# Attention scores of two heads: one product over 128 rows, or two of 64 rows side by side

## The chip, the cores and the metric

The kernel runs on one core of one Trainium2 chip, in one launch. The metric is the device time of an execution in microseconds (us). TensorE multiplies: it loads a tile of weights (stationary) and streams columns of the other operand past it, into PSUM banks of 2 KB per partition. VectorE, ScalarE and GpSimd work on the results; SyncE issues the DMAs. Each engine runs its own queue in order and waits on semaphores for the others.

## What is computed

The reference is a stack of two attention layers followed by two layers of a mixer and a feed-forward part, for one sequence of 256 tokens with 1024 channels. Only the attention layers matter here. Each has three kinds of attention with 64 channels a head: 4 heads that see a selection of keys (dsa), 6 heads with a decay by cumulated gates (fox), and 6 heads that are used three times, on compressed, selected and windowed keys (nsa; the compressed branch is computed elsewhere).

```
s = jnp.einsum("bthd,bshd->bhts", qb, k).astype(jnp.float32) * scale
s = s + cb[:, :, :, None] - cum[:, :, None, :]        # fox only
p = masked_softmax(s, causal)
return jnp.einsum("bhts,bshd->bthd", p.astype(v.dtype), v)
```

All attention is causal, so the first 128 queries see 128 keys and the second 128 see 256.

## The kernel before, in words

`attend` does one pair of heads: 2 calls for dsa, 3 for fox and 6 for nsa (two branches of three pairs) in each layer, 22 calls in all. The queries of both heads lie stacked on 128 partitions, 64 channels each. The keys `kp` are laid out as a block diagonal of `[128, 2, 256]`: head 0 has its keys on rows 0 to 63 of its half and zeros below, head 1 zeros above and its keys on rows 64 to 127. One product of 128 rows thus gives both heads' scores next to each other in one PSUM bank.

A call goes through two token blocks `tb`. For each: the score product (L813; 256 columns for block 0, 512 for block 1, float32, two records each in the trace since a float32 product is made in two passes); for fox the decay (L816, one product per head); the mask as a bfloat16 product with the identity (L818, or L821 for dsa with its own mask); the row maximum of both heads in one VectorE instruction (L823); an exponential with its row sum on ScalarE for each head (L826); the reciprocal and the scaling on VectorE (L827, L831); transposes of the probabilities on TensorE (L835) and their copy to SBUF (L836). After both blocks come the products with the values (L839, L841), two heads in the two column halves of the array. The scores use the PSUM tag `s`, which has two banks; block 0 takes one and block 1 the other, and `turn` (L803) and the norm (L586) use the same tag.

Around this stand the projections of the layer: 16 units of `w_in` (L457, L458, L462 and L493: each weight is split into a high and a low part by ScalarE, L436, and VectorE, L437, and multiplied in three products) and then `w_out` (L510). They do not depend on the attention, so a scheduler in the recording layer puts them between the steps of `attend`; it decides by priorities and its own costs in which order instructions stand in each engine's queue. On the chip the queues then run in that order whatever the times. `self.after` adds an order between two instructions without a wait.

Lines used below that are not about scores: L1586 is a product of 64 rows in the mixer's recurrence, L1123 one in the compression of keys, and L412 with `oht` a product of 64 rows in the expert stage; L1162, L919 and L657 are small products near the attention.

Of the kernel before, what the change touches and what calls it, by code (L numbers as in the profile page):

```python
# [15 lines left out]
AF = mybir.ActivationFunctionType  # L16
ALU = mybir.AluOpType
AX = mybir.AxisListType
# [264 lines left out]
class Net:  # L283
# [522 lines left out]
    def attend(self, o, q, kp, vs, bias=None, first=True, last=True, cum=None, gate=None):  # L806

        nc = self.nc
        pt = self.hw.tile([128, 2, 384], F32, name="pt", tag="pt")
        for tb in range(2):  # L810
            K = 128 * (tb + 1)
            s = self.psum("s")[:, :2 * K].rearrange("p (a k) -> p a k", a=2)
            nc.tensor.matmul(s, q[:, tb * 128:tb * 128 + 128], kp[:, :, :K], start=True, stop=False)  # L813
            if cum is not None:
                for a in range(2):
                    nc.tensor.matmul(s[:, a], self.onehot(cum + a), self.cumt[:, :K], start=False, stop=False)  # L816
            if bias is None:
                nc.tensor.matmul(s[:, :, K - 128:], self.identb, self.mask[:, None].to_broadcast([128, 2, 128]), start=False,  # L818
                                 stop=True)
            else:  # L820
                nc.tensor.matmul(s, self.identb, bias[tb], start=False, stop=True)  # L821
            st = self.sm.tile([128, 6], F32, name="st")
            nc.vector.tensor_reduce(st[:, 0:2], s, axis=AX.X, op=ALU.max, negate=True)  # L823
            p = self.hw.tile([128, 2, K], F32, name="p", tag=f"p{tb}", bufs=2)
            for a in range(2):
                nc.scalar.activation(p[:, a], s[:, a], AF.Exp, bias=st[:, a:a + 1], accum_out=st[:, 2 + a:3 + a])  # L826
            nc.vector.reciprocal(st[:, 4:6], st[:, 2:4])  # L827
            if gate is not None:
                nc.vector.tensor_tensor(st[:, 4:6], st[:, 4:6], gate[:, tb], op=ALU.mult)
            for a in range(2):  # L830
                nc.vector.tensor_scalar(p[:, a], p[:, a], st[:, 4 + a:5 + a], None, op0=ALU.mult)  # L831
            pp = self.psum("t")[:, :2 * K].rearrange("p (a k) -> p a k", a=2)
            for a in range(2):
                for kb in range(tb + 1):
                    nc.tensor.transpose(pp[:, a, kb * 128:kb * 128 + 128], p[:, a, kb * 128:kb * 128 + 128], self.ident)  # L835
            nc.scalar.copy(pt[:, :, tb * 128:tb * 128 + K], pp)  # L836
        for a in range(2):
            r = slice(64 * a, 64 * a + 64)
            nc.tensor.matmul(o[r, :], vs[a](0), pt[:, a, 0:256], start=first, stop=False, skip_group_check=True,  # L839
                             tile_position=(0, 64 * a))  # L840
            nc.tensor.matmul(o[r, 128:256], vs[a](1), pt[:, a, 256:384], start=False, stop=last,  # L841
                             skip_group_check=True, tile_position=(0, 64 * a))
# [1369 lines left out]
```

## Time and profile before

| | us |
|---|---|
| median of 3 runs (lowest to highest) | 1862.64 (1861.03 to 1862.64) |
| the profiled execution, its own time | 1859.58 |
| its span, first to last instruction | 1857.7 |
| TensorE matmul busy in the span | 1788.7 |
| VectorE busy | 1069.8 |
| ScalarE busy | 873.2 |

A matmul's duration in the trace runs from its start to the end of its way through the array, and the next one starts earlier; what a product costs in the queue is therefore read from one start to the next. Weight loads have rows of their own (PEld) and overlap products. The two attention layers lie at about 0 to 235 us and 240 to 425 us, the score products from 97 to 211 and from 265 to 396; the last 800 us are the expert stage, which streams its weights by DMA.

### The profile page before, as it was taken

The page shows a single profiled execution, that of the slowest core. Times are in us where ns is not written, and L with a number is a line of the kernel's source. Part 1 is how long each engine was busy: PE and PEld are TensorE (multiplying, and loading weights), DVE is VectorE, ACT ScalarE, POOL GpSimd, SP SyncE. Part 2 cuts the span into 40 slices and gives each one's busy share as a digit, 9 for nine tenths or more (in the row PEclk, how much of TensorE's full clock was granted, in tenths as well). Part 3 has the DMA queues.
Part 4 walks back from the last instruction along what each step waited for, and adds up shares of the span by engine and source line. Part 5 has one row for each costly group of instructions (what it writes and reads, how often), then busy time and mean ns, then how long its engine had stood idle before and what let it go on. Part 6 is the DMA issues. An engine that isn't in the chain of part 4 may idle for free. (4 is left out here: it accounts for less than half of the span.)

```text
span 1857.7 us, 27558 instructions
## 1 busy us (share of the span) xinstructions
PE 1788.7 (96%) x11038; PEld 1357.8 (73%) x11038; DVE 1069.8 (58%) x1570; ACT 873.2 (47%) x1295; POOL 33.1 (2%) x78
## 2 busy tenths in 40 slices
PE   7999999999999999999999999888999999999996
PEld 5777788778897999888977876665666565656552
DVE  3765688757644655466437855645556555646532
ACT  3455475545463444355446754444444444544421
POOL 1000010000000000000000000000000000000000
PEclk9999999999999999999998999989999999999998
DMA  9664443234211555543137989999999999999996
GB/s 387 252 227 162 180 160 125 69 115 171 92 68 58 193 182 182 182 149 114 46 114 291 343 343 420 421 420 421 421 419 415 420 421 420 416 421 421 410 386 263
DMA packets 71175, 497.71 MB, mean 268 GB/s; under 512 B 8226, under 2 KB 9538, under 8 KB 11264
## 3 DMA queue, kind: packets, MB, share of 16 engines
q1 hardware_dynamic: 70752, 495.39, 67.9%
q8 instruction: 89, 1.46, 0.3%
q0 software_dynamic: 288, 0.48, 0.1%
q14 instruction: 46, 0.38, 0.1%
HBM read 493.81 MB, written 1.05 MB: 266 GB/s over the span
## 5 line engine op out<-in xcount | busy, mean ns | idle before, releaser
L437 DVE TENSOR_TENSOR raw<-raw,whi 128x2048 fp32r<-128x2048 f32 (+1 forms) x161 | 288.7, 1812 | 183.0 <-ACT whi L436 182.1
L436 ACT CAST whi<-raw 128x2048 fp32r<-128x2048 f32 (+1 forms) x188 | 287.1, 1552 | 155.8 <-PE mm L458 48.6
L412 PE MATMUL mm<-room,fx 128*64 128x512 f32 (+1 forms) x560 | 177.8, 535 | 12.1 <-DMA room<-in_mup_dram 6.3
L457 PE MATMUL mm<-xhi,whi 128*128 128x256 f32 x720 | 182.1, 288 | 0.7 <-ACT whi L436 0.7
L412 PE MATMUL mm<-whi,gh 128*128 128x512 f32 x448 | 177.7, 397 | 3.6 <-DVE y L2004 2.0
L458 PE MATMUL mm<-xlo,whi 128*128 128x256 f32 x720 | 180.4, 286 | 0.0
L412 PE MATMUL mm<-raw,fx 128*64 128x512 f32 (+1 forms) x544 | 171.9, 531 | 7.2 <-DMA raw<-in_mup_dram 7.2
L412 PE MATMUL mm<-whi,gl 128*128 128x512 f32 x448 | 174.9, 390 | 0.0
L436 ACT CAST whi<-room 128x2048 fp32r<-128x2048 f32 (+1 forms) x84 | 148.9, 1788 | 34.5 <-PE s L412 10.4
L457 PEld LDWEIGHTS mm<-xhi,whi 128*128 128x128 f32 x720 | 137.8, 191 | 8.1 <-issue 5.6
L458 PEld LDWEIGHTS mm<-xlo,whi 128*128 128x128 f32 x720 | 137.8, 191 | 1.5 <-issue 1.4
L412 PE MATMUL s<-whi,mh 128*128 128x512 f32 x448 | 116.5, 402 | 0.0
L412 PEld LDWEIGHTS s<-whi,mh 128*128 128x128 f32 x448 | 82.3, 188 | 35.5 <-issue 17.5
L462 PE MATMUL mm<-xhi,raw 128*128 128x256 f32 x720 | 104.6, 285 | 0.0
L412 PEld LDWEIGHTS mm<-room,fx 128*64 128x64 f32 (+1 forms) x560 | 54.5, 131 | 67.8 <-issue 44.1
L412 PEld LDWEIGHTS mm<-whi,gh 128*128 128x128 f32 x448 | 84.2, 188 | 21.5 <-issue 4.6
L412 PEld LDWEIGHTS mm<-whi,gl 128*128 128x128 f32 x448 | 84.2, 188 | 16.8
L412 PEld LDWEIGHTS mm<-raw,fx 128*64 128x64 f32 (+1 forms) x544 | 52.0, 131 | 59.5 <-issue 42.7
L462 PEld LDWEIGHTS mm<-xhi,raw 128*128 128x128 f32 x720 | 93.7, 192 | 1.2 <-DVE cin L1218 0.9
L1933 ACT CAST mh<-t 128x512 fp32r<-128x512 f32 x28 | 16.4, 586 | 159.6 <-PE t L415 159.6
L437 DVE TENSOR_TENSOR room<-room,whi 128x2048 fp32r<-128x2048 f32 x32 | 73.3, 2290 | 29.2 <-ACT whi L436 28.0
L412 PE MATMUL o<-room,msg 128*64 128x512 f32 (+1 forms) x536 | 85.5, 508 | 1.0 <-DVE msg L1928 1.0
(585 smaller groups left out, 3323.0 us busy)
## 6 DMA issues: line engine op xcount, KB each, us to landing
room<-in_mdown_dram SPq DMA_DIRECT2D x79, 1024.0 KB, 16.6
room<-in_mup_dram SPq DMA_DIRECT2D x54, 1024.0 KB, 17.0
room<-in_mgate_dram SPq DMA_DIRECT2D x53, 1024.0 KB, 13.9
raw<-in_mgate_dram SPq DMA_DIRECT2D x44, 1024.0 KB, 16.2
raw<-in_mup_dram SPq DMA_DIRECT2D x41, 1024.0 KB, 15.5
raw<-in_win_dram SPq DMA_DIRECT2D x29, 1024.0 KB, 6.3
raw<-in_din_dram SPq DMA_DIRECT2D x24, 1024.0 KB, 4.9
raw<-in_ada_dram SPq DMA_DIRECT2D x22, 1024.0 KB, 10.9
```

The costliest lines, as they stand in the source:

```text
L412: return self.kept(self.nc.tensor.matmul(*a, **k))
L436: a = nc.scalar.copy(h[:, v], r[:, v])
L437: b = nc.vector.tensor_tensor(lo[:, v], r[:, v], h[:, v].bitcast(F32), op=ALU.subtract)
L457: nc.tensor.matmul(out, w, xh[:, k], start=start and i == 0, stop=False)
L458: nc.tensor.matmul(out, w, xl[:, k], start=False, stop=False)
L462: nc.tensor.matmul(out, lo[:, off + i * 128:off + i * 128 + 128], xh[:, k], start=False, stop=stop and i == n - 1)
L1933: i = nc.scalar.copy(hh, pt), nc.vector.tensor_tensor(hl, pt, hh.bitcast(F32), op=ALU.subtract)
```

## The change

Each head gets a product of its own with 64 rows: head 0 on rows 0 to 63 of the array, head 1 on rows 64 to 127, without the zeros of the block diagonal. Each head has a PSUM bank of its own, which holds block 0 in columns 0 to 127 and block 1 in columns 128 to 383, so both banks belong to one call from its first product to its last exponential. Masks become one product a head, maxima one instruction a head, and each exponential follows its head's maximum.

```
+        ss = [self.psum("s") for _ in range(2)]
+        opened = [None, None]
         for tb in range(2):
             K = 128 * (tb + 1)
-            s = self.psum("s")[:, :2 * K].rearrange("p (a k) -> p a k", a=2)
-            nc.tensor.matmul(s, q[:, tb * 128:tb * 128 + 128], kp[:, :, :K], start=True, stop=False)
-            if cum is not None:
-                for a in range(2):
-                    nc.tensor.matmul(s[:, a], self.onehot(cum + a), self.cumt[:, :K], start=False, stop=False)
-            if bias is None:
-                nc.tensor.matmul(s[:, :, K - 128:], self.identb, self.mask[:, None].to_broadcast([128, 2, 128]), start=False,
-                                 stop=True)
-            else:
-                nc.tensor.matmul(s, self.identb, bias[tb], start=False, stop=True)
+            s = [t[:, 128 * tb:128 * tb + K] for t in ss]
+            for a in range(2):
+                r = slice(64 * a, 64 * a + 64)
+                m = nc.tensor.matmul(s[a], q[r, tb * 128:tb * 128 + 128], kp[r, a, :K], start=tb == 0, stop=False,
+                                     tile_position=(64 * a, 0), skip_group_check=True)
+
+                self.after(m, opened[a])
+                opened[a] = m
+            for a in range(2):
+                if cum is not None:
+                    nc.tensor.matmul(s[a], self.onehot(cum + a), self.cumt[:, :K], start=False, stop=False,
+                                     skip_group_check=True)
+                if bias is None:
+                    nc.tensor.matmul(s[a][:, K - 128:], self.identb, self.mask, start=False, stop=True, skip_group_check=True)
+                else:
+                    nc.tensor.matmul(s[a], self.identb, bias[tb][:, a], start=False, stop=True, skip_group_check=True)
             st = self.sm.tile([128, 6], F32, name="st")
-            nc.vector.tensor_reduce(st[:, 0:2], s, axis=AX.X, op=ALU.max, negate=True)
             p = self.hw.tile([128, 2, K], F32, name="p", tag=f"p{tb}", bufs=2)
             for a in range(2):
-                nc.scalar.activation(p[:, a], s[:, a], AF.Exp, bias=st[:, a:a + 1], accum_out=st[:, 2 + a:3 + a])
+                nc.vector.tensor_reduce(st[:, a:a + 1], s[a], axis=AX.X, op=ALU.max, negate=True)
+                nc.scalar.activation(p[:, a], s[a], AF.Exp, bias=st[:, a:a + 1], accum_out=st[:, 2 + a:3 + a])
```

The new lines shift those below by nine (L835 becomes L844). In the changed kernel the score product is L818, the decay L825, the masks L828 and L830, the maximum L834, the exponential L835, the transposes L844.

The first place is TensorE's queue at the first dsa call of layer 0. Before, both blocks' products and masks stand together:

```order
L493 MATMUL mm<-whi,xlo 128x256 x5
L813 MATMUL s<-kp_dk,q_dq_695 128x256
L821 LDWEIGHTS identb
L821 MATMUL s<-dsab_677,identb 128x256
L813 MATMUL s<-kp_dk,q_dq_695 128x512
L821 LDWEIGHTS identb
L821 MATMUL s<-dsab_680,identb 128x512
L493 MATMUL mm<-whi,xlo 128x256 x3
```

The same place of the changed kernel on TensorE:

```order
L493 MATMUL mm<-whi,xlo 128x256 x5
L818 MATMUL s<-kp_dk,q_dq_695 128x128 x2
L830 LDWEIGHTS identb
L830 MATMUL s<-dsab_677,identb 128x128
L830 LDWEIGHTS identb
L830 MATMUL s<-dsab_677,identb 128x128
L493 MATMUL mm<-whi,xlo 128x256 x3
L493 MATMUL mm<-raw_1140,xhi 128x256 x5
L818 MATMUL s<-kp_dk,q_dq_695 128x256 x2
L844 MATMUL t<-lead,p 128x128 x2
L830 LDWEIGHTS identb
L830 MATMUL s<-dsab_680,identb 128x256
```

Both heads' products are next to each other (x2); block 1 has moved behind eight projection products, and block 0's transposes stand between its products and its masks.

The second place is TensorE's queue at block 1 of the windowed branch of the first nsa pair. Before:

```order
L835 MATMUL t<-lead,p 128x128 x2
L458 MATMUL mm<-xlo,whi 128x256
L813 MATMUL s<-keys,q_rq_1217 128x512
L818 LDWEIGHTS identb
L818 MATMUL s<-mask,identb 128x2x128
```

The same call and block in the changed kernel:

```order
L462 MATMUL mm<-xhi,raw_1667 128x256 x6
L818 MATMUL s<-keys,q_rq_1223 128x256
L844 MATMUL t<-lead,p 128x128 x4
L818 MATMUL s<-keys,q_rq_1223 128x256
L828 LDWEIGHTS identb
L828 MATMUL s<-mask,identb 128x128
L828 LDWEIGHTS identb
L828 MATMUL s<-mask,identb 128x128
L462 MATMUL mm<-xhi,raw_1667 128x256 x2
```

Here the two heads' products are apart, with four transposes of full size between them.

## Rows read from the trace of the kernel before

**Rows 1.** The windows: length, then busy time (instructions) by engine, clock, DMA share, GB/s.

```profile
core 0: us, PE busy (x) PEld busy (x) DVE busy (x) ACT busy (x) POOL busy (x), PEclk, DMA share, GB/s
95.00:220.00 125.00, 123.63 (x953) 97.67 (x953) 78.16 (x159) 65.62 (x161) 0.00 (x0) 1.00 0.51 192
260.00:425.00 165.00, 163.03 (x1138) 134.72 (x1136) 119.92 (x284) 92.02 (x212) 1.70 (x3) 1.00 0.33 112
425.00:1060.00 635.00, 624.33 (x4137) 549.21 (x4135) 366.05 (x607) 312.08 (x524) 15.19 (x19) 0.98 0.43 154
1060.00:1857.00 797.00, 759.69 (x3878) 477.97 (x3876) 423.29 (x316) 343.26 (x290) 2.56 (x3) 0.98 0.97 402
```

**Rows 2.** The waits of TensorE in 95:425: total us, times, longest; first and last.

```profile
PE s L813 <- ACT q_fq L1029: 0.9, 2, 0.7
...
PE o L839 <- ACT pt L836: 0.2, 1, 0.2
```

**Rows 3.** The timeline of TensorE at the first call: start, length, instruction.

```profile
97.15 0.67 PE L813 MATMUL s<-kp_dk,q_dq 128*128 128x256 f32 x2
97.66 0.27 PE L821 MATMUL s<-dsab,identb 128*128 128x256 bf16 x1
97.77 1.02 PE L813 MATMUL s<-kp_dk,q_dq 128*128 128x512 f32 x2
98.63 0.38 PE L821 MATMUL s<-dsab,identb 128*128 128x512 bf16 x1
```

**Rows 4.** The timeline of one block 0 from mask to exponential, in 207.3:209.2.

```profile
207.10 0.39 PE L816 MATMUL s<-cumt,lead 128*128 128x128 f32 x2
...
207.32 0.27 PE L818 MATMUL s<-mask,identb 128*128 128x256 bf16 x1
...
207.63 0.42 DVE L823 TENSOR_REDUCE st<-s 128x2 f32<-128x256 f32 x1 [0.50 <-PE s L818]
...
208.09 0.37 ACT L826 ACTIVATE p<-s,st 128x128 f32<-128x128 f32 x1 [0.37 <-DVE st L823]
...
208.45 0.36 ACT L826 ACTIVATE p<-s,st 128x128 f32<-128x128 f32 x1
```

**Rows 5.** The timeline of TensorE in the expert stage, around 1493.5.

```profile
1493.53 1.20 PE L412 MATMUL mm<-my,oht 64*128 64x512 f32 x8
```

**Rows 6.** The timeline of TensorE around a product of 64 rows, 561.24:562.9.

```profile
561.24 0.39 PE L510 MATMUL mm<-whi,xhi 128*128 128x512 f32 x1
561.47 0.40 PE L510 MATMUL mm<-raw,xhi 128*128 128x512 f32 x1
561.79 0.48 PE L1586 MATMUL s<-vn,kbd 64*128 64x128 f32 x2
562.21 0.73 PE L510 MATMUL mm<-whi,xlo 128*128 128x512 f32 x2
562.78 0.40 PE L510 MATMUL mm<-whi,xhi 128*128 128x512 f32 x1
```

**Rows 7.** The timeline of TensorE around another, 86.8:88.1.

```profile
86.54 0.52 PE L493 MATMUL mm<-raw,xhi 128*128 128x256 f32 x3
86.90 0.28 PE L493 MATMUL mm<-whi,xhi 128*128 128x256 f32 x1
87.11 0.40 PE L1123 MATMUL t<-ch,cw 64*128 64x30 f32 x2
87.44 0.85 PE L493 MATMUL mm<-whi,xhi 128*128 128x256 f32 x5
```

**Rows 8.** Groups of weight loads in 95:425: busy us, mean ns, idle before.

```profile
L457 PEld LDWEIGHTS mm<-xhi,whi 128*128 128x128 f32 x224 | 42.7, 191 | 2.9 <-issue 1.9
...
L835 PEld LDWEIGHTS t<-lead,p 128*128 128x128 f32 x132 | 14.8, 140 | 9.8 <-issue 5.0 <-ACT pt L836 3.1 <-PE s L818 0.8
```

**Rows 9.** Line L818 by itself, the mask's weight load: ns min/median/max.

```profile
L818 PEld LDWEIGHTS <-identb x36: 97/98/181, 127.9 to 393.6; 128*128 128x128 bf16 x36
```

**Rows 10.** Line L823 by itself, the maxima: ns min/median/max.

```profile
L823 DVE TENSOR_REDUCE st<-s x44: 415/546/693, 98.0 to 394.2; 128x2 f32<-128x256 f32 x22, 128x2 f32<-128x512 f32 x22
```

**Rows 11.** VectorE's costliest group in 95:425, the weight split.

```profile
L437 DVE TENSOR_TENSOR raw<-raw,whi 128x2048 fp32r<-128x2048 f32 x35 | 80.1, 2289 | 42.5 <-ACT whi L436 42.5
```

## Prediction

> **What bounds the kernel now.** I read the windows first, since the change touches only the two attention layers. In the two stretches that hold their score products TensorE is busy 123.63 of 125.00 us and 163.03 of 165.00 us at a granted clock of 1.00, while VectorE is busy 78.16 and 119.92 and DMA moves at 0.51 and 0.33 of its share [rows 1]. So TensorE bounds these stretches and the other engines stand beside it. The table of waits says the same from the other side: in 95:425 TensorE's named waits are eight lines, from 0.9 us down to 0.2 us, 4.7 us in all [rows 2]. TensorE runs in order and has hardly a hole there, so a nanosecond added to its queue is a nanosecond added to the kernel. Behind these layers lie a stretch where TensorE is busy 624.33 of 635.00 us, and the expert stage, where DMA has 0.97 of its share [rows 1]. That stage cannot take back a late start: its loads go into buffers that earlier work frees, and moved by a later start they end as much later. I count TensorE's change in full.
>
> **What goes.** One attend has a score product for token block 0 (256 columns) and one for block 1 (512 columns). From the start of each to the start of the mask behind it: 97.15 to 97.66, 0.51 us, and 97.77 to 98.63, 0.86 us [rows 3]. 22 attends: 22 x 1.37 = 30.1 us go.
>
> **What comes: the products themselves.** A 64-row product of one head has half the columns. Two passes over 128 columns take 0.22 us (207.10 to 207.32 [rows 4]), two over 256 take 0.43 us (half of 0.86 [rows 3]). If the two heads stand next to each other in TensorE's queue they can run at once: in the expert stage eight records of 64 rows and 512 columns, on two row halves, take 1.20 us [rows 5], where 0.23 us apart, as full products start (561.24, 561.47 [rows 6]), they would need 1.8 us. I take the second head at 0.01 us for its start. Bounds: 0 and its full length.
> But the heads are next to each other in only half of the places. Counting score products in the changed queue: of the 44 pairs of heads 8 of block 0 and 13 of block 1 stand side by side; the other 23 are split by a mask, by transposes or by projection products (the second place shown under the change has four transposes in between). That leaves 36 uses of 0.22 us (8 pairs, 28 singles) and 31 of 0.43 us (13 pairs, 18 singles): 7.9 + 13.3 + 0.2 = 21.4 us.
>
> **What comes: switching the array.** Every one of these 67 groups is an island of 64-row work in a queue of 128-row work, and the trace shows the price. L1586 is a float32 product of 64 rows and 128 columns alone between full products. From 561.47 to 562.78 [rows 6] lie three full products (0.23 us each, as from 561.24 to 561.47) and L1586's own two passes (0.22 us): 0.91 us of work in 1.31 us. The island costs 0.40 us over its work: 0.09 before it, 0.20 from its start to the next full product, 0.11 on that product, whose weight load nothing hides. A second island is near it: from 86.90 to 87.44 [rows 7] lie one product of 0.12 us (86.54 to 86.90 holds three) and two passes of 30 columns, 0.05 us by L1586's width: 0.37 us over the work, and then the late load.
> What follows an island here is mostly the mask, whose bfloat16 weight load is short: 98 ns [rows 9] against 191 for a float32 one [rows 8]; these 36 cost 0.40 - 0.09 = 0.31 us. 16 are followed by a transpose (load of 140 ns [rows 8]: 0.35 us), the other 15 by float32 loads (0.40 us): mean 0.34 us. An island with its mask behind is not in the trace; its bounds are 0.1 (the entry wait alone) and 0.5 (the second island's price, rounded up). Islands of other shapes (values, gates, compressed keys) were there before: counting every change of tile size from shortly before the first score product to past the last one gives 94 before and 221 now. So 127 changes are new, 63.5 islands: 63.5 x 0.34 = 21.6 us.
> The Trainium skill, "TensorEngine Tiling (Array Packing)", Key Properties, says that changing the tiling mode drains TensorE, which is the rule that speaks against this change; it gives no price, and rows 6 do. The same page, Theoretical Speedup, gives up to 2x for a contraction of 64 rows or fewer; that alone would bring half of the 30.1 us, 15 us, and has its place among the rivals.
>
> **What comes: masks.** Two mask products of 128 columns replace one of 256: 0.11 us in either form (97.66 to 97.77 [rows 3]). But a half mask of 0.055 us covers only half of the 0.11 us that the next float32 weight load takes; where such a load follows (some 53 times) 0.055 us shows: 2.9 us. Bounds 0 and 5.
>
> **What comes: waits.** Block 1 now writes into the banks that block 0's exponentials read, so a bank is one round of mask, maximum, exponential. From rows 4: mask at 207.32, maximum at 207.63, which at half the width takes 0.29 us in place of 0.42 (an estimate from 0.42 and 0.69 for the two widths [rows 10]), exponential 0.37, so 1.0 us for the first head and, 0.36 later, 1.4 for the second; with 256 columns 1.25 and 1.75. What stands between on TensorE is mostly 8 projection products (0.96 us), transposes or value products. Laid end to end with the row times, four places come up short, 0.7 us in all. A weight split of 2.29 us on VectorE [rows 11] in front of a maximum can lengthen it; the projection products queued behind the waiting score product on TensorE, and ScalarE's and VectorE's later work on them, then wait as well. I take 2 us, bounds 0 and 12 (0.27 us a round).
> **Beside other work.** 44 more maxima on VectorE: 22 x (0.42 + 0.69) = 24 us become 44 x (0.29 + 0.42) = 31 us. VectorE is busy 0.63 to 0.73 of these stretches [rows 1], so TensorE hides the 7 us; without that cover they would be the price. The exponentials are the same in number and size. DMA issues, GpSimd and all stages after attention keep their order.
>
> **Sum.** -30.1 + 21.4 + 21.6 + 2.9 + 2 = +17.8 us. The profiled execution took 1859.58 us (span 1857.7), so 1877.4 by its own clock; the median of the runs is 3.1 us above it, and 1862.6 + 17.8 gives **1880 us**. The island decides the size: each 0.1 us of its price is 6.4 us.
>
> **Rivals.** (A) Switching to row halves waits for nothing: islands cost no more than their work. Then the sum is -30.1 + 21.4 + 2.9 + 2 = -4 us: 1859, a little faster; it turns slower once an island costs over 0.06 us. This is the skill page's speedup as far as the queue allows it (15 us only if all 44 pairs stood side by side). For it: rows 5, where halves overlap well. Against it: rows 6 and 7, the same shape of island in this same program.
> (B) The halves don't overlap in float32, whose products have two passes each with its own weight load: 8 x 0.22 + 13 x 0.43 = +7 us more, 1888. For it: rows 6 show one half at a time only, and rows 5 are one-pass products. Against it: rows 5 interleave several loads on both halves.
> (C) The bank round becomes the bound: in each attend block 1 waits out most of block 0's 1.4 us because weight splits stand in front: 22 x 1.2 = 26 us in place of 2, 1904. For it: maxima and splits share VectorE's queue, and a split takes 2.29 us [rows 11]. Against it: rows 2, where the waits that the queue had planned for came to 0.9 us at most.
> (D) The expert stage takes the delay back: it lives on DMA (0.97 [rows 1]), and if its loads start by themselves, TensorE's late arrival costs nothing: 1863. For it: DMA has only 0.43 of its share in the stretch before, room to run ahead. Against it: the loads need buffers that TensorE empties, and TensorE is busy 759.69 of 797.00 us in that stage too, so it has little to catch up with.
>
> **Chances.** Forecast 0.75 (own range 1872 to 1888), B 0.08, C 0.07, A 0.05, D 0.05. The range 1868 to 1891 takes in B and most of the bounds on the island (0.2 to 0.5 us) and leaves out A, C and D. A measurement of this kernel tells 0.2%, 3.7 us, from no change: faster 0.03 and same 0.07 (A on both sides of that line, and D), slower 0.90.
>
> **What would show it.** In the changed profile a lone score product of 128 columns should stand some 0.5 us from what precedes it to what follows beyond its neighbours' usual spacing, and two heads in a row should start within 0.02 us of each other. The attention stretches should be longer by 7 to 11 us each with TensorE as busy as before, the stages behind unchanged in length. VectorE's maxima rise to 88 without TensorE waiting for them. I am wrong if an island costs under 0.2 us, if TensorE's named waits before score products grow to over 5 us, or if the stages behind absorb the delay.

## The result, and the profile after

The changed kernel took 1876.93 us (median of four runs, 1872.33 to 1881.01) where the kernel before took 1861.84 beside it (1860.90 to 1862.64). The ratio is 1.0082 [1.0065, 1.0099]: 15.1 us slower. Forecast were +17.8 us and slower, with 1868 to 1891 as the range.

The profiled execution of the changed kernel is the longest of its four runs (1881.01 us, span 1879.2). The windows of both kernels, cut at the same places of the program (the transposes of the norm behind the first attention layer, the mixers' first product behind the second, the start of the expert stage), say where the time went. Columns: stretch, length, TensorE busy (instructions), granted clock, DMA share, GB/s. The kernel before:

```profile
core 0: us, PE busy (x), PEclk, DMA share, GB/s
95.00:230.51 135.51, 133.69 (x996) 1.00 0.52 194
230.51:429.53 199.02, 195.06 (x1373) 1.00 0.36 123
429.53:1070.17 640.64, 630.70 (x4167) 0.98 0.44 155
1070.17:1857.70 787.53, 749.52 (x3823) 0.98 0.98 404
```

The changed kernel:

```profile
core 0: us, PE busy (x), PEclk, DMA share, GB/s
95.00:238.11 143.11, 142.29 (x1060) 1.00 0.50 183
238.11:444.93 206.82, 203.00 (x1439) 1.00 0.34 118
444.93:1087.07 642.14, 632.21 (x4168) 0.97 0.44 155
1087.07:1879.20 792.13, 752.42 (x3823) 0.97 0.97 401
```

The first attention layer is 7.6 us longer and the second 7.8, 15.4 us together, at a clock of 1.00 (2.4 GHz) in both kernels. The stages behind do the same work (4167 and 3823 instructions, one record more or less); their 1.5 and 4.6 us came at a granted clock of 0.97 for 0.98. The other three runs of this kernel were 2 to 9 us shorter, and its median is 15.1 us behind, so I take these 6 us for what single executions differ by. The nine profiled executions bear that out: from the mixers' first product to the end they take 1427.8 to 1434.3 us, 1428.0 in the kernel that comes latest to it (heads apart, below) and 1432.9 in one whose TensorE work is that of before (maxima a head). The length of TensorE's stretch less its busy time, summed over both layers, was 1.82 + 3.96 = 5.8 us and is 0.82 + 3.82 = 4.6.

The waits of TensorE in 95:440 (total us, times, longest), which answer to [rows 2]; all six lines together make 3.8 us, and none names a score product:

```profile
PE s L586 <- DVE n L583: 1.1, 2, 0.6
PE o L493 <- ACT whi L436: 0.7, 1, 0.7
...
PE s L803 <- DVE rot L793: 0.3, 1, 0.3
```

Two heads side by side, in the timeline of TensorE around 130 us, answer to [rows 3]; the second fence is one of the places where they don't run at once, with the exponential that frees the bank (the last two rows are from narrow windows, where only the passes in the window are counted). PEld is TensorE's weight loader, and ACTIVATION_READ_ACCUMULATOR is the reading of the exponential's row sum.

```profile
129.44 0.39 PE L657 MATMUL mm<-raw,crep 128*32 128x256 f32 x3
129.76 0.49 PE L818 MATMUL s<-keys,q_rq 64*128 64x128 f32 x4
130.18 0.23 PE L828 MATMUL s<-mask,identb 128*128 128x128 bf16 x1
```

```profile
113.21 0.28 PE L458 MATMUL mm<-xlo,whi 128*128 128x256 f32 x1
113.33 0.37 ACT L835 ACTIVATE p<-s,st 128x128 f32<-128x128 f32 x1 [0.41 <-DVE st L834]
113.42 1.12 PE L818 MATMUL s<-kp_dk,q_dq 64*128 64x256 f32 x4
113.60 0.19 ACT L835 ACTIVATION_READ_ACCUMULATOR p<-s,st 128x1 f32 x1
...
114.47 0.10 PEld L830 LDWEIGHTS <-identb 128*128 128x128 bf16 x1 [0.33 <-issue]
...
113.42 0.70 PE L818 MATMUL s<-kp_dk,q_dq 64*128 64x256 f32 x2
113.84 0.70 PE L818 MATMUL s<-kp_dk,q_dq 64*128 64x256 f32 x2
```

At 129.76 all four passes of both heads are over in 0.42 us (to the mask at 130.18); the two heads' first passes start 6 ns apart. At 113.42 head 0 makes both of its passes alone and head 1 starts at 113.84. That is 0.05 us after the end, at 113.79, of block 0's exponential, which began at 113.33 and reads the bank that head 1 is to write. The pair takes 1.05 us to the mask instead of 0.63 for a pair of this width that runs at once. Of the 21 pairs that stand side by side in the queue, 14 start within 0.03 us of each other and 7 lie 0.2 to 0.42 us apart.

The score product's line by itself, loads and products, and what ended the idle time of the weight loader before it (us, times; two of the lines):

```profile
L818 PEld LDWEIGHTS s<-keys,q_rq x96: 182/184/187, 129.8 to 371.6; 64*128 64x128 f32 x96
L818 PE MATMUL s<-keys,q_rq x96: 272/375/480, 129.8 to 371.9; 64*128 64x128 f32 x48, 64*128 64x256 f32 x48
...
  issue: 4.8, 22
  ACT p L835: 1.7, 7
```

The maxima, by width (busy us, mean ns, idle before), answer to [rows 10]:

```profile
L834 DVE TENSOR_REDUCE st<-s 128x1 f32<-128x256 f32 x44 | 17.3, 419 | 14.3 <-PE s L828 12.7 <-PE s L830 1.3
L834 DVE TENSOR_REDUCE st<-s 128x1 f32<-128x128 f32 x44 | 12.1, 287 | 21.0 <-PE s L828 16.6 <-PE s L830 4.2
```

### The profile page after: what moved, and what is told of

The parts are those of the page before. It is cut to its first block, busy times and chain, and to the rows that moved or that the text cites. A ratio compares the mean times of both kernels' runs of the same rounds, so it can differ in the third digit from the quotient of the medians.

```text
span 1879.2 us, 27855 instructions
## 1 busy us (share of the span) xinstructions
PE 1809.6 (96%) x11170; PEld 1367.3 (73%) x11170; DVE 1074.9 (57%) x1614; ACT 875.5 (47%) x1295; POOL 33.1 (2%) x78
## 3 DMA queue, kind: packets, MB, share of 16 engines
HBM read 493.81 MB, written 1.05 MB: 263 GB/s over the span
```

## Experiments

The theory was the prediction's sum: a piece of 64-row work between 128-row work (an island) costs some 0.34 us beyond its work, and the overlap of the heads brings back less. The rivals were that the two heads don't overlap, that the time lies in the other parts of the edit (more instructions, the bank a head), and that any short product put into these places would cost as much. Every kernel was timed in five rounds beside runs of the kernel before (1861.11 us for the first four, 1862.41 for the others). "Changes" below are changes of tile size in TensorE's queue over the attention layers: 94 before, 221 in the changed kernel.

**All 128 rows again.** The changed kernel with its banks, masks and maxima a head, but each head's product over all 128 rows of the block diagonal: 99 changes.

```
-  nc.tensor.matmul(s[a], q[r, tb * 128:tb * 128 + 128], kp[r, a, :K], ..., tile_position=(64 * a, 0), ...)
+  nc.tensor.matmul(s[a], q[:, tb * 128:tb * 128 + 128], kp[:, a, :K], ...)
```

> The changed kernel, but each head's score product takes all 128 rows of the block diagonal (one head's half of the columns), so no change of tile size comes with it; banks, masks, maxima and the places of the 88 products in TensorE's queue stay those of the changed kernel. Tile changes in the attention fall from 221 to 99 (before: 94). Islands decide: the products cost 44 x 0.22 + 44 x 0.43 = 28.6 us, near the 30.1 of before, the half masks 2.9 and the waits up to 2, so +1 to +5 us on before, 1863 to 1867. The bank round decides: the delay stays, +13 us or more, 1875. No overlap of halves tells nothing here.

Measured: 1866.39 us, ratio 1.0028 [1.0012, 1.0043]. Two thirds of the loss are gone with the 64-row tiles; the rest of the edit (two products a block, two masks, two maxima, a bank a head) costs about 5 us (2 to 8 by the interval), at the top of what was expected.

Both kernels have the same 67 groups of score products between the same neighbours in TensorE's queue, so they can be compared place by place. One lone product of 128 columns with 64 rows, then with 128:

```profile
112.11 0.28 PE L458 MATMUL mm<-xlo,whi 128*128 128x256 f32 x1
112.32 0.49 PE L818 MATMUL s<-kp_dk,q_dq 64*128 64x128 f32 x2
112.74 0.23 PE L830 MATMUL s<-dsab,identb 128*128 128x128 bf16 x1
```

```profile
111.85 0.28 PE L458 MATMUL mm<-xlo,whi 128*128 128x256 f32 x1
111.96 0.39 PE L818 MATMUL s<-kp_dk,q_dq 128*128 128x128 f32 x2
112.19 0.22 PE L830 MATMUL s<-dsab,identb 128*128 128x128 bf16 x1
```

From the product ahead to the mask behind it is 0.63 us with 64 rows and 0.34 with 128, so this island costs 0.29 us. Less the 0.11 between full products, the 0.63 is the 0.5 us that the prediction named as its sign. The starts of the single passes split it: 0.09 before the first pass, 0.10 between the two passes (0.21 us apart instead of 0.11), 0.09 behind the second.

**A bare island.** The kernel before with one product of 64 rows and one column, of zeros, ahead of each of its 44 score products: 176 changes, 41 islands.

```
+  m = nc.tensor.matmul(s[:, 0, 0:1], q[0:64, tb * 128:tb * 128 + 128], kp[0:64, 1, 0:1], start=True, ...,
+                       tile_position=(0, 0), ...)
...
```

> The kernel before, with one product of 64 rows and one column (a column of zeros of the block diagonal) put ahead of each of the 44 score products, into the same bank. It adds no maximum, no mask, no bank and no work to speak of: only islands, 82 more changes of tile size (94 to 176). Islands decide: 41 x (0.40 + 0.04 for two passes of one column) = +18 us, 1880. Switching is free: +2 us, 1864. Bank round: +2 us as well, since the banks are used as before.

**The same product without the change of tile.** The control: one column of zeros, but over all 128 rows; 93 changes.

```
+  m = nc.tensor.matmul(s[:, 0, 0:1], q[:, tb * 128:tb * 128 + 128], self.c["causal"][:, 0:1], start=True, ...)
...
```

> The control of e2_bare_island: the kernel before with the same kind of one-column product of zeros ahead of each of the 44 score products, but over all 128 rows, so that no change of tile size comes with it (93 changes, 94 before). What an island costs beside the switch is the weight load that a short product does not hide: two passes of 0.11 us each (the spacing of one-column products elsewhere in this program is 0.112 us), 44 x 0.22 = +10 us, 1871. Then the switch itself is what e2 has on top, (17.4 - 9.7) / 41 = 0.19 us an island, as read from the starts before and after L1586 (0.09 and 0.09). If the whole price of e2 was the switch, this one costs next to nothing: +2 us, 1863.

Measured: 1878.55 us for the island, 1.0089 [1.0072, 1.0106], and 1868.14 for the control, 1.0031 [1.0021, 1.0042]. The timelines of TensorE show both at the second block of the first call, the kernel with the island first (here L813 is the added product, L815 the score product, L824 the masks ahead of it and behind it):

```profile
98.47 0.27 PE L824 MATMUL s<-dsab,identb 128*128 128x256 bf16 x1
98.67 0.38 PE L813 MATMUL s<-kp_dk,q_dq 64*128 64x1 f32 x2
98.98 1.13 PE L815 MATMUL s<-kp_dk,q_dq 128*128 128x512 f32 x2
99.95 0.38 PE L824 MATMUL s<-dsab,identb 128*128 128x512 bf16 x1
```

```profile
97.12 0.27 PE L824 MATMUL s<-dsab,identb 128*128 128x256 bf16 x1
97.22 0.28 PE L813 MATMUL s<-const,q_dq 128*128 128x1 f32 x2
97.37 1.10 PE L815 MATMUL s<-kp_dk,q_dq 128*128 128x512 f32 x2
98.31 0.38 PE L824 MATMUL s<-dsab,identb 128*128 128x512 bf16 x1
```

From the mask to the score product behind it lay 0.11 us before (97.66 to 97.77 [rows 3]), 0.51 with the island, 0.25 with the control. From that mask to the next one it was 0.97 us before (97.66 to 98.63), 1.48 with the island, 1.19 with the control. So here the island costs 0.40 us at the start of the score product and 0.51 at the mask behind that, the control 0.14 and 0.22. Timed over all places, the island costs 0.0089 x 1861 = 16.6 us, 0.40 for each of the 41, and the control 0.0031 x 1862 = 5.8, 0.13 for each of its 44 products. The two differ in the tile: 0.26 to 0.29 us in these rows, and 10.8 / 41 = 0.26 by the times (0.17 to 0.35 by their intervals), is the price of going to 64 rows and back. What is left I take for two weight loads of a product too short to hide them; no run separates them. The control was expected at +10 us, 0.22 for each product. This place shows that price, but all of them together came to less. The switch was expected at 0.19 us of the island's price; by the rows it is the larger part, and the times alone would still allow 0.19.

"TensorEngine Tiling (Array Packing)" of the Trainium skill, Key Properties, says that a change of tiling mode drains TensorE. The island's rows agree, with a delay on either side of it (0.20 us from mask to island where the control has 0.11, and 0.31 from the island to the next product where the control has 0.14); the price is this run's.

**Heads kept apart.** The changed kernel with head 0's decay and mask between the two heads' products: 259 changes, 88 lone products, no overlap.

```
             for a in range(2):
...
-                self.after(m, opened[a])
-                opened[a] = m
-            for a in range(2):
+                self.after(m, opened[a] if a == 0 else done)
...
+                    done = nc.tensor.matmul(s[a][:, K - 128:], self.identb, self.mask, ...)
                 else:
+                    done = nc.tensor.matmul(s[a], self.identb, bias[tb][:, a], ...)
+                opened[a] = m
```

> The changed kernel with each head's decay and mask put between the two heads' score products, so that no two products of 64 rows stand side by side: 88 lone products instead of 46 lone and 21 pairs, 259 changes of tile size instead of 221. Islands with overlap in the pairs: 19 islands at 0.31 to 0.34 us = 6.2 us, and the overlap of 21 pairs is lost, 8 x 0.22 + 13 x 0.43 = 7.3 us: +13 us on the changed kernel, 1890. Islands but no overlap of halves in float32: +6 us, 1883. Bank round: heads are no further behind each other than before, near 1877.

Measured: 1890.90 us, 1.0164 [1.0147, 1.0180]: 30 us over the kernel before, 14 over the changed kernel by the medians. Had the heads not overlapped in the changed kernel (rival B), keeping them apart would have cost the 19 further islands, 6.5 us at 0.34; the rest is lost overlap and what new waits there are. A lone product in TensorE's timeline:

```profile
96.54 0.49 PE L818 MATMUL s<-kp_dk,q_dq 64*128 64x128 f32 x2
96.95 0.23 PE L828 MATMUL s<-dsab,identb 128*128 128x128 bf16 x1
97.11 0.48 PE L818 MATMUL s<-kp_dk,q_dq 64*128 64x128 f32 x2
```

One head alone takes 0.42 us to its mask (96.54 to 96.95), which is what two heads took together at 129.76.

**One island a call.** If islands cost and overlap pays, a call should have one island with everything in it. The masks (one product a head for both blocks; for dsa one a block) and decays come first (they open the banks), then all four 64-row products of both blocks follow each other: 131 changes, 22 groups.

```
+  for a in range(2):
...
+          done = nc.tensor.matmul(both, self.identb, self.mask[:, None].to_broadcast([128, 2, 128]), start=True, ...)
...
+  with self.ahead(20000):
+      for tb in range(2):
+          for a in range(2):
+              m = nc.tensor.matmul(s[a], q[r, ...], kp[r, a, :K], start=False, stop=True,
+                                   tile_position=(64 * a, 0), ...)
+              self.after(m, done)
```

> The same two 64-row products a block and a bank a head, but the masks and decays go first and the four products of a call follow as one group with nothing between: 22 islands in place of 67 (131 changes of tile size, 94 before), all 44 pairs side by side, masks of 256 columns. Islands with overlap: products 22 x (0.22 + 0.43) + 0.4 = 14.7 us for 30.1, 18.5 new islands at 0.40 us = 7.4 us, waits 0 to 4: -8 to -4 us on before, 1854 to 1858. Islands but no overlap: +14.3 more, 1868 to 1872. Bank round: each bank is now held through both blocks' exponentials, so a call waits longer than in the changed kernel: 1880 or more.

**The same order without islands.** As the last kernel, with all 128 rows in each of the four products: 96 changes.

> e4_one_island with full rows: masks and decays first, the four products of a call together, a bank a head, but each product over all 128 rows of the block diagonal, so no islands and no overlap (96 changes of tile size). Islands with overlap: products 28.6 us as in e1, masks of 256 columns and no half masks, waits 0 to 4: -1 to +3 us on before, 1860 to 1864; e4 is then better by the overlap (13.9 us) less its islands (7.4 us), 6 us. If e4 gained by its order and banks alone, this one is as fast as e4, 1856. If the banks held through both blocks cost something that the overlap of e4 hides, 1866 or more.

Measured: 1855.99 us for one island a call, 0.9974 [0.9965, 0.9984], which is faster than both the kernel before and the changed one (by 21 us); and 1859.93 for the same order without islands, 0.9982 [0.9972, 0.9992]. TensorE's timeline at the first call, with 64-row products (L832, behind the masks L821) and then with 128-row ones:

```profile
97.97 0.33 PE L821 MATMUL s<-dsab,identb 128*128 128x128 bf16 x2
98.22 0.93 PE L832 MATMUL s<-kp_dk,q_dq 64*128 64x128 f32 x8
99.08 0.50 PE L493 MATMUL mm<-whi,xlo 128*128 128x256 f32 x2
```

```profile
97.06 0.33 PE L821 MATMUL s<-dsab,identb 128*128 128x128 bf16 x2
97.22 1.47 PE L832 MATMUL s<-kp_dk,q_dq 128*128 128x128 f32 x8
98.35 0.59 PE L493 MATMUL mm<-whi,xlo 128*128 128x256 f32 x2
```

The windows of the two attention layers in the same order:

```profile
95.00:228.23 133.23, 131.27 (x1048) 1.00 0.53 197
228.23:424.07 195.84, 191.87 (x1422) 1.00 0.36 125
```

```profile
95.00:229.10 134.10, 133.28 (x1042) 1.00 0.52 195
229.10:427.36 198.26, 194.98 (x1421) 1.00 0.36 123
```

Four products of 64 rows take 0.86 us to the next product, four of 128 rows 1.13 us. Counted from the masks ahead, and so with the whole switch, it is 1.11 and 1.29 us: with the heads in pairs and one switch for four products, the 64-row form is shorter in the trace. The page of the Trainium skill named above gives up to 2x for a contraction of 64 rows or fewer (Theoretical Speedup). This group stays below that, at 1.13 / 0.86 = 1.3 and 1.29 / 1.11 = 1.2 with its switch, and the changed kernel, with 67 groups, has a loss.

The island order's layers are 329.07 us against 332.36 without islands and 334.53 before. These windows begin at 95 us, where the island order already ran 0.9 us behind the other; counted from the first product of the key selection (`s<-ikp,q_iq`, at 58.5, 57.6 and 58.1 us), which none of the edits touches, they take 365.55, 369.75 and 371.46. By this place 22 x 0.27 = 5.9 us were to be had from row halves, and the layers show 3.3 to 4.2: TensorE's idle time is 5.9 us in the one and 4.1 in the other, so 1.8 us went into waits. Expected was a lead of 6 us; by the ratios it is 0.0008 of 1862, 1.5 us, and their intervals overlap, so the times do not show the lead and the traces alone do. The order without islands is also faster than the kernel before, by 3.4 us (1.5 to 5.2), where a change of -1 to +3 us was expected. How the gain divides between order and row halves stays open: the order has two thirds of it by the ratios and less than half in the layers (1.7 of 5.9 us from the common product).

**Maxima a head.** The kernel before with one maximum a head instead of one for both.

```
-  nc.vector.tensor_reduce(st[:, 0:2], s, axis=AX.X, op=ALU.max, negate=True)
...
   for a in range(2):
+      nc.vector.tensor_reduce(st[:, a:a + 1], s[:, a], axis=AX.X, op=ALU.max, negate=True)
       nc.scalar.activation(p[:, a], s[:, a], AF.Exp, ...)
```

> The kernel before with the maximum of each head as its own VectorE instruction, followed by its exponential, and nothing else changed: 44 more instructions, 7 us more on VectorE. Hidden beside TensorE, as forecast: within 2 us of before, 1859 to 1863. If VectorE's queue sets the pace of TensorE (the bank round's theory), up to +7 us, 1868.

Measured: 1861.38 us, 0.9995 [0.9984, 1.0006]. VectorE's 44 further instructions are hidden by TensorE.

## Why the prediction was right

- **What bounds the kernel.** TensorE does: it is busy 142.29 of 143.11 and 203.00 of 206.82 us of the two attention layers. What is added to its queue there is added to the kernel, and the later stages gave nothing back (rival D): the windows behind have the same instructions and are no shorter, and the kernel with the heads apart came to them 29 us late and took 1428.0 us from there, as the kernel before did (1428.2).
- **Islands, 0.34 us each, the term that decides.** The mechanism holds. Rival A (switching is free) is excluded: it would have left the bare island within a few us of the control. The size is read best against the kernel with all 128 rows. There the 46 lone products take 0.29 us less in the median from the instruction ahead to the next one, where the step had 0.31 with a mask behind; the mean is 0.25, since some stand beside other small tiles that were there before, and at some the 128-row product waits too. Together the lone products make +11.4 us, the 14 pairs that run at once -1.8 and the 7 late ones +0.4: 10.0 us, or 13.0 when read two instructions further on. Measured, the changed kernel's profiled execution reached the mixers at 444.93 us and the kernel with all 128 rows at 433.12, 11.8 us apart. The forecast for this was 21.6 for the islands less 7.2 of halved work (44 products of 0.22 and 44 of 0.43 us, 28.6 us, became 21.4), 14.4 us. The bare island's 0.40 us is not the price of these islands: the control, a product of one column without a change of tile, pays 0.14 of it too, so its agreement with [rows 6] confirms little.
- **Overlap in 21 of 44 pairs.** The mechanism holds: first passes 6 ns apart, four passes in 0.42 us, and rival B is excluded by the kernel that keeps the heads apart. But the step took every such pair to start "within 0.02 us of each other"; 12 of 21 do, 2 start 23 and 26 ns apart, and 7 between 0.2 and 0.42 us. Measured to the next instruction, the seven cost 2.1 us: one pair of 128 columns 0.81 us where 0.42 is usual, six of 256 columns 0.93 in the mean where 0.64 is.
- **Waits, 2 us, bounds 0 and 12.** Wrong in form, and right in size by luck. In six of the seven late pairs head 1 of block 1 does wait for block 0's exponential in the bank that both blocks share: its weight load starts 0.05 us after ScalarE is done (the pairs at 98.89, 113.42, 183.38, 208.59, 214.75 and 318.09; the one at 96.85 waits for an earlier work of ScalarE, q_nq, L943). But TensorE as a whole is not idle: head 0 goes ahead and head 1 comes late, so the price is a lost overlap, 2.1 us, and TensorE's table of waits shows none of it. The seven waits of the weight loader for the exponential (1.7 us, L818 above) are not these pairs: all stand before the first load of a group, and only the one at 208.59 is in a late pair. Rival C (26 us) is far off.
- **Maxima.** 88 of them, 0.287 and 0.419 us where 0.29 and 0.42 were estimated, at no cost: the separate run says the same.
- **Masks, 2.9 us.** Not taken apart. The kernel with all 128 rows holds this term and the second product's in its 5 us.
- **The sum.** +17.8 us forecast; +15.4 in the two layers of the profiled execution, +15.1 by the medians. In two parts: the change to 64 rows was forecast at 14.4 us and measured at 11.8; the rest of the edit was forecast at -1.5 + 2.9 + 2 = 3.4 us (the products 28.6 for 30.1, the masks, the waits) and measured at 3.6 (the mixers at 433.12 us for 429.53) or 5 by the times. So the miss, 2.6 us, lies in the change to 64 rows, whose islands were priced somewhat high. Where exactly stays open; single executions differ by about as much before the attention starts (the kernel with maxima a head made its first product of the key selection at 55.8 us, the kernel before at 58.1).

## What to carry to other kernels

Price a smaller tile by its islands, not by its columns: count in the queue how often the tile size changes, take the price from a lone product of that size in the trace, and compare it with what the overlap can save in the pairs that really stand side by side. If row halves are used at all, put all of them behind one switch, with every bank they write free before the first starts, since a second half that waits for its bank runs alone. And try the new order with full tiles too: here it was faster than the kernel before by itself, and only the traces, not the times, tell the row halves from it.

## What the runs showed of the hardware

- A lone 64-row float32 product of 128 columns takes 0.63 us between its neighbours, where the same product over 128 rows takes 0.34. The price of the smaller tile lies before its first pass (0.09), between its two passes (0.10) and behind them (0.09).
- A float32 product of a single column over 128 rows, with next to nothing to stream, still delays the next product by 0.14 us and the mask behind that by 0.22.
- Halves of the rows interleave by pass: in the group of four products the eight passes start in pairs 6 or 7 ns apart, though each float32 pass has its own load. A half whose bank is not free starts late by itself (6 of 21 pairs, by 0.2 to 0.42 us).
- The longer runs of the changed kernel are those with the lower mean granted clock (a mean between the levels 1.2 and 2.4 GHz): it took 1872.33 and 1875.09 us at 0.986 and 1878.78 and 1881.01 at 0.980, and its expert stage took 792.13 us at 0.97, where the kernel with one island a call took 787.05 at 0.99 with the same 3823 instructions:

```profile
1067.05:1854.10 787.05, 745.85 (x3823) 0.99 0.98 404
```

What the engine did before the clock differed was not followed up.
